# A hybrid convolution / RWKV-7 layer on one core: the score blocks' transposition cut in four, the weights' low parts made in two halves

## The chip, the core and the metric

The kernel runs on one core of one Trainium2 chip. A core has five engines that work side by side, each through its own list of instructions in order: TensorE (PE, matrix products; its weight loads are shown apart as PEld), VectorE (DVE), ScalarE (ACT), GpSimd (POOL) and SyncE (SP), which issues the transfers. The metric is the device time of one execution in microseconds, lower is better; the span in the profile is the time from the first to the last instruction of one profiled execution.

## The reference

One layer of a decoder is computed for 2048 new tokens of one sequence and for 8 short sequences of 4 tokens, which come with states. All is fp32, the model width is 1024:

```python
h = _rmsnorm(x, norm_g)
p = jnp.einsum('bsd,dn->bsn', h, w_in)
p_conv, p_rwkv, p_gate = _split(p, [N_CONV_COLS, N_RWKV_COLS, 2 * D_MODEL])
...
def step(S, inp):
    r_t, k_t, v_t, d_t, kk_t, a_t = inp
    sa = jnp.einsum('bhvk,bhk->bhv', S, -kk_t)
    S = (S * d_t[:, :, None, :] + sa[..., None] * (kk_t * a_t)[:, :, None, :]
         + v_t[..., None] * k_t[:, :, None, :])
    y = jnp.einsum('bhvk,bhk->bhv', S, r_t)
    return S, y
...
m = jax.nn.sigmoid(gc) * pc + jax.nn.sigmoid(gr) * pr
out = jnp.einsum('bsd,de->bse', m, w_o)
return x + out, new_conv, h[:, -1], S_fin.astype(S0.dtype)
```

A big projection feeds a gated convolution and an RWKV-7 branch of 16 heads, whose state is a 64 x 64 matrix for each head that every token decays and changes. Two output projections are gated, added, and projected once more.

## The kernel before, in words

**Precision.** A large product is done as three passes of a fast fp32 format: each operand X is split into a rounded high part and the rest, a low part, and high times high, low times high and high times low are added. For a weight block of 1024 x 128 the high part is a copy on ACT and the low part a subtraction on DVE (`whl<-wraw,whl` in the profile, `w_lows`). The first time a block is used both parts are stored to memory (`SP.store(keep, ...)`); the later sets read them back. There are 105 such subtractions, 81 of them for the input projection, most in the first quarter of the time.

**Sets, pairs, chunks.** The 2048 tokens are taken in four sets of 512; the last one also carries the short sequences. A set goes through 8 pairs of heads, so there are 32 pairs in all, and the recurrence of a pair runs over 8 chunks of 64 tokens. Inside a chunk the recurrence is rewritten with matrix products, and that needs the inverse of a lower triangular matrix of 64 x 64 for each head and chunk.

**The main stream.** PE's bulk is the projections (matmuls into `ip`, 24 for each block of 128 columns: 8 parts of the depth, three passes). `main_stream` walks them.

**The sides.** All other work is written as generators, which yield a weight after each step: `rwkv_keys` makes the scaled keys of a pair, `rwkv_solve` the inverse, `rwkv_merge` and `rwkv_load` put it and the transposed operands in place, `rwkv_chain` runs the eight chunks, `rwkv_out` normalises. They run one pair behind each other: while the chain of one pair runs, the inverse of the next one is solved. `drive` gives each side as much as its weight asks for after each projection matmul, if the planner (`Clock`, a running estimate of when each engine is free) says that what it needs is ready. So PE's order comes out as projections with small matmuls of the sides in between. The planner's costs for DVE depend on the number of elements, so more or smaller instructions shift its estimate and with it the places where the sides are let in. Afterwards the framework's own scheduler moves independent instructions of one engine past each other; what stands in the built program is shown below.

**The inverse.** In `rwkv_solve` two groups of score matmuls (`pt<-AR,BK`) are masked on DVE (`GM<-pt,mask_p`), ACT packs the diagonal blocks of 32 x 32 of eight chunks, two heads and two halves in `Mc`, and one DVE transposition of 128 x 1024 turns it into `Mi` (`Mi<-Mc`). Then 31 steps of a substitution follow on DVE, from row j = 31 down to 1, each with two instructions: a product (`tt<-Mi,X`), which reads row j of `Mi`, and a sum (`X<-X,tt`). A last transposition gives `Xo`.

**The chain.** Each chunk of `rwkv_chain` goes back and forth: PE multiplies the state (`pa<-S,AR`), DVE adds (`us<-pa,P`, two halves), PE multiplies with the inverse (`pb<-us,Xbd`), DVE and then ACT copy a half of the result each (`SV<-pb`), PE multiplies with the keys (`pb<-SV,BKt`), DVE updates the state (`S<-pb,pe,sp`, two halves), and the next chunk begins. Between two of these matmuls PE has only the projections that stand between them in its list.

Every operation is recorded through one helper, so all have line 121 in the profile; tiles tell them apart.

Of the kernel before, what the change touches and what calls it, by code (L numbers as in the profile page):

```python
# [7 lines left out]
F32 = mybir.dt.float32  # L8
# [3 lines left out]
ALU = mybir.AluOpType  # L12
# [4 lines left out]
P = 128  # L17
# [4 lines left out]
NCH = 8  # L22
# [4 lines left out]
W = {"sq": 1.0, "norm": 1.0, "lora": 2.0, "one": 1.0, "scan": 2.0, "exp": 2.0, "key": 1.0, "bones": 1.5,  # L27
     "sv": 1.5, "bt": 2.0, "score": 4.0, "inv0": 5.0, "inv": 0.45, "inv1": 4.0, "merge": 2.0,
     "gk": 1.3, "us": 1.3, "sa": 1.3, "state": 1.3, "samp": 2.0, "gn": 4.0, "out": 2.0}
# [150 lines left out]
def hybrid_kernel(tc, x_prompt, x_sample, state_conv, state_shift, state_rwkv, norm_g, w_in, conv_w,  # L180
# [5 lines left out]
    V, A, G, T = (Traced(e, n, clock) for e, n in ((nc.vector, "DVE"), (nc.scalar, "ACT"), (nc.gpsimd, "POOL"), (nc.tensor, "PE")))  # L186
# [4 lines left out]
    NB = D // P  # L191
# [57 lines left out]
    def w_lows():  # L249
        while lows:  # L250
            hl, raw, keep = lows.pop(0)
            V.tensor_tensor(out=hl[:, 1], in0=raw, in1=hl[:, 0].bitcast(F32), op=ALU.subtract)
            SP.store(keep, hl.bitcast(F32))

    def take_w(key):

        i = state["use"]
        assert order[i][0] == key, (order[i][0], key)
        state["use"] += 1
        w_advance(i + 1, i + 1, i + 1)  # L260
        w_lows()
        SP.flush(2)
        w_advance(i + 3, i + 2, i + WAHEAD)
        return parts_.pop(i)
# [211 lines left out]
    for q in range(2):  # L476
        V.tensor_tensor(out=mask_s[:, q, 0:NSAMP].rearrange("p (j i) -> p j i", i=SL),
                        in0=mask_p[:, q, 0:NSAMP].rearrange("p (j i) -> p j i", i=SL),
                        in1=seqm.unsqueeze(2).broadcast_to([P, NS, SL]), op=ALU.mult)
# [450 lines left out]
    def rwkv_solve(th, p, o):  # L930

        AR = o["AR"]
        samp = th == LAST
        GM = GMB[(th * NB + p) % 2]


        yield 0.0, (), 2
        for c0 in range(0, NCH + samp, 4):
            cs = range(c0, min(NCH + samp, c0 + 4))
            pp = [new_pt([P, 512], F32, name="pt") for _ in range(2)]  # L940
            for c in cs:
                for h in range(2):
                    T.matmul(pp[h][:, (c - c0) * P:(c - c0 + 1) * P], lhsT=BK[HS[h], c].rearrange("p q t -> p (q t)"),
                             rhs=AR[HS[h], c].rearrange("p q t -> p (q t)"), start=True, stop=True)
            k = len(cs)
            mk = mask_s if c0 == NCH else mask_p
            for h in range(2):
                V.tensor_tensor(out=GM[:, c0:c0 + k, :, h, :],
                                in0=pp[h][:, 0:k * P].rearrange("p (c a t) -> p c a t", a=2, t=64),
                                in1=mk.unsqueeze(1).broadcast_to([P, k, 2, 64]), op=ALU.mult)  # L950
            yield W["score"], (), 2 if c0 + 4 < NCH + samp else 0


        Mc = rw.tile([P, NCH, 32], F32, name="Mc")
        for i, g in enumerate(blk):
            h, b = i // 2, slice(i % 2 * 32, i % 2 * 32 + 32)
            A.copy(Mc[g], GM[b, 0:NCH, 0, h, b])
        yield 0.5, [Mc]
        Mi = rw.tile([P, 32, 32], F32, name="Mi")
        V.transpose(Mi.rearrange("p t (e c) -> p t e c", c=NCH),  # L960
                    Mc.rearrange("p c t -> p t c").unsqueeze(2).broadcast_to([P, 32, 4, NCH]))
        X = rw.tile([P, 8, 32], F32, name="X")
        A.copy(X, X0)
        Mo = rw.tile([P, NCH, 32], F32, name="Mo")
        A.copy(Mo[64:96], GM[0:32, 0:NCH, 0, 1, 32:64])
        yield W["inv0"], [Mi, X]

        for j in range(31, 0, -1):
            c0 = j // 4
            tt = sm.tile([P, 80], F32, name="tt")  # L970
            tv = tt[:, 0:(8 - c0) * j].rearrange("p (c i) -> p c i", i=j)
            V.tensor_tensor(out=tv, in0=Mi[:, j, 0:j].unsqueeze(1).broadcast_to([P, 8 - c0, j]),
                            in1=X[:, c0:8, j:j + 1].broadcast_to([P, 8 - c0, j]), op=ALU.mult)
            V.tensor_tensor(out=X[:, c0:8, 0:j], in0=X[:, c0:8, 0:j], in1=tv, op=ALU.add)
            yield W["inv"]
        Xo = rw.tile([P, 8, 4, 8], F32, name="Xo")
        V.transpose(Xo.rearrange("p a e c -> p (a e c)"), X.rearrange("p a b -> p (a b)"))
        o.update(GM=GM, Xo=Xo, Mo=Mo)
        yield W["inv"]
# [315 lines left out]
    for th in range(NSETS):  # L1295
        for p in range(NB):
            last = p == NB - 1
            k = 6 if th < LAST else (5 if not last else len(cg[th]))
# [143 lines left out]
    for th, hv, p, nx in plan:  # L1442
# [11 lines left out]
        e = EDGE / 2 * NB  # L1454
# [161 lines left out]
```

## Time and profile before

| what | value |
|---|---|
| median of 3 runs | 3207.14 us (3201.25 to 3209.92) |
| the profiled execution's own time | 3209.42 us |
| its span | 3207.7 us |
| PE busy | 3102.1 us (97%) |
| DVE busy | 1999.0 us (62%) |
| ACT busy | 1241.4 us (39%) |
| POOL busy | 309.9 us (10%) |
| mean granted TensorE clock | 0.991 |

PE is busy nearly all the time, so the time is PE's work and, beside it, the 105.6 us of the span (3207.7 - 3102.1) in which PE waited. A busy DVE costs nothing by itself; it costs where PE's next matmul waits for it. The columns of a group's row are: line, engine, operation, tile written <- tiles read, shapes, count | busy us, mean ns of one | idle us of the engine just before, and what ended it. In a timeline the first column is the start in us, the second the duration.

### The profile page before, as it was taken

How to read it: one execution, taken by the hardware profiler on the slowest of the kernel's cores; microseconds unless marked ns; L12 is line 12 of the kernel's file. 1: busy time of each engine (PE TensorE's matmuls, PEld its weight loads, DVE VectorE, ACT ScalarE, POOL GpSimd, SP SyncE). 2: the span in 40 equal slices, each digit the busy share in tenths (PEclk: the TensorE clock that was granted, in tenths of full speed). 3: DMA queues.
4: the chain of work that ended last, by engine and by line, in shares of the span. 5: the costliest groups of instructions: out<-in, count | busy, mean ns of one | idle time of the engine just before them, and what ended most of it. 6: DMA issues, size and time to landing. Idle time of an engine off the chain costs nothing. (4 is left out here: it accounts for less than half of the span.)

```text
span 3207.7 us, 55738 instructions
## 1 busy us (share of the span) xinstructions
PE 3102.1 (97%) x21594; PEld 2603.2 (81%) x21594; DVE 1999.0 (62%) x5712; ACT 1241.4 (39%) x2571; POOL 309.9 (10%) x517
## 2 busy tenths in 40 slices
PE   7999999999999999999999999999999999999998
PEld 6777777877777778777777799988898889778897
DVE  5687777776666666666666666776677654443332
ACT  5454554444433344444443444434344432211201
POOL 2011111110000001001110010000000000000000
PEclk9999999999999999999999999999999999999999
DMA  8786666644444444444444444343443469988863
GB/s 267 256 274 211 216 221 218 204 171 151 144 157 155 161 159 159 168 151 158 159 157 151 160 152 138 134 136 129 143 138 126 144 217 311 350 338 305 316 245 120
DMA packets 240991, 615.10 MB, mean 192 GB/s; under 512 B 33418, under 2 KB 143107, under 8 KB 186966
## 3 DMA queue, kind: packets, MB, share of 16 engines
q1 hardware_dynamic: 240582, 611.00, 55.5%
q8 instruction: 171, 2.80, 0.4%
q14 instruction: 94, 0.77, 0.1%
q0 software_dynamic: 144, 0.52, 0.0%
HBM read 452.10 MB, written 159.36 MB: 191 GB/s over the span
## 5 line engine op out<-in xcount | busy, mean ns | idle before, releaser
L121 PE MATMUL ip<-XH,whl 128*128 128x512 f32 (+3 forms) x7776 | 2107.3, 351 | 10.2 <-DVE gt L121 3.5
L121 PEld LDWEIGHTS ip<-XH,whl 128*128 128x128 f32 x7776 | 1341.8, 190 | 184.2 <-issue 30.4
L121 PE MATMUL ip<-XL,whl 128*128 128x512 f32 (+3 forms) x3888 | 1362.9, 351 | 2.6 <-POOL XL L121 2.6
L121 PEld LDWEIGHTS ip<-XL,whl 128*128 128x128 f32 x3888 | 738.5, 190 | 77.4 <-issue 6.2
L121 DVE TENSOR_TENSOR X<-X,tt 128x60 f32<-128x60 f32 (+24 forms) x992 | 211.7, 213 | 27.4
L121 DVE TENSOR_TENSOR tt<-Mi,X 128x60 f32<-128x60 f32 (+24 forms) x992 | 210.5, 212 | 28.0
L121 DVE SCALAR_TENSOR_TENSOR S<-pb,pe,sp 64x64 f32<-64x64 f32 x512 | 143.7, 281 | 100.7 <-PE pb L121 94.6
L121 ACT ACTIVATE sp<-S,pe 128x128 f32<-128x128 f32 x256 | 99.5, 399 | 264.2 <-DVE S L121 260.7
L121 ACT ACTIVATE tmp<-ip,vec 128x512 f32<-128x512 f32 (+2 forms) x174 | 103.2, 593 | 232.5 <-PE ip L121 231.1
L121 ACT COPY SV<-pb 64x64 f32<-64x64 f32 x256 | 53.3, 208 | 330.9 <-DVE SV L121 326.9
L121 PE MATMUL po<-whl,MH 128*128 128x512 f32 x544 | 170.6, 394 | 2.6 <-ACT whl L121 2.5
L121 DVE TENSOR_TENSOR whl<-wraw,whl 128x1024 fp32r<-128x1024 f32 x105 | 134.2, 1279 | 52.8 <-ACT whl L121 52.5
L121 DVE TENSOR_TENSOR us<-pa,P 64x64 f32<-64x64 f32 x512 | 110.3, 215 | 51.9 <-PE pa L121 39.8
L121 PEld LDWEIGHTS pb<-us,Xbd 128*128 128x128 f32 x512 | 86.3, 190 | 54.4 <-PE ip L121 20.8
L121 PE MATMUL ip<-RH,whl 128*128 128x512 f32 (+2 forms) x512 | 128.5, 341 | 1.1 <-DMA whl<-w_or 0.6
L121 PEld LDWEIGHTS pb<-SV,BKt 128*128 128x128 f32 x512 | 85.2, 189 | 54.0 <-ACT SV L121 45.3
L121 ACT CAST whl<-wraw 128x1024 fp32r<-128x1024 f32 x105 | 109.4, 1044 | 43.9 <-DMA wraw<-in_w_out_r_dram 14.0
L121 PEld LDWEIGHTS po<-whl,MH 128*128 128x128 f32 x544 | 102.1, 188 | 27.0 <-ACT whl L121 2.9
L121 PE MATMUL pb<-SV,BKt 128*128 128x128 f32 x512 | 107.1, 291 | 16.4 <-ACT SV L121 16.1
L121 DVE TENSOR_TENSOR GM<-pt,mask_p 128x512 f32<-128x512 f32 x128 | 82.4, 686 | 61.4 <-PE pt L121 61.4
L121 PE MATMUL pb<-us,Xbd 128*128 128x64 f32 x512 | 90.1, 258 | 22.5 <-DVE us L121 21.9
L121 ACT COPY Xbd<-Xo 32x256 f32<-32x256 f32 x128 | 88.2, 689 | 61.2 <-DVE Xo L121 59.1
(494 smaller groups left out, 3856.1 us busy)
## 6 DMA issues: line engine op xcount, KB each, us to landing
wraw<-in_w_in_dram SPq DMA_DIRECT2D x81, 512.0 KB
whl<-w_k SPq DMA_DIRECT2D x24, 1024.0 KB
whl<-w_r SPq DMA_DIRECT2D x24, 1024.0 KB
whl<-w_v SPq DMA_DIRECT2D x24, 1024.0 KB
whl<-w_z SPq DMA_DIRECT2D x24, 1024.0 KB
whl<-w_xin SPq DMA_DIRECT2D x24, 1024.0 KB
whl<-w_cg SPq DMA_DIRECT2D x24, 1024.0 KB
whl<-w_zc SPq DMA_DIRECT2D x24, 1024.0 KB
```

Source lines behind the costliest of these rows:

```text
L121: r = f(*a, **k)
```

## The change

In `w_lows` the low part of a weight block is made by two subtractions of 128 x 512 in place of one of 128 x 1024. In `rwkv_solve` the transposition of 128 x 1024 is cut in four of 128 x 256, each of which makes eight rows of `Mi` and is written into the loop of the substitution just ahead of the first step that reads one of them (j = 31, 23, 15 and 7). The weight that the transposition had for the planner, 5, is given out in five parts.

```diff
@@ w_lows
             hl, raw, keep = lows.pop(0)
-            V.tensor_tensor(out=hl[:, 1], in0=raw, in1=hl[:, 0].bitcast(F32), op=ALU.subtract)
+            for k in range(2):
+                c = slice(k * (NB // 2) * P, (k + 1) * (NB // 2) * P)
+                V.tensor_tensor(out=hl[:, 1, c], in0=raw[:, c], in1=hl[:, 0, c].bitcast(F32), op=ALU.subtract)
             SP.store(keep, hl.bitcast(F32))
@@ rwkv_solve
         Mi = rw.tile([P, 32, 32], F32, name="Mi")
-        V.transpose(Mi.rearrange("p t (e c) -> p t e c", c=NCH),
-                    Mc.rearrange("p c t -> p t c").unsqueeze(2).broadcast_to([P, 32, 4, NCH]))
         X = rw.tile([P, 8, 32], F32, name="X")
         A.copy(X, X0)
         Mo = rw.tile([P, NCH, 32], F32, name="Mo")
         A.copy(Mo[64:96], GM[0:32, 0:NCH, 0, 1, 32:64])
-        yield W["inv0"], [Mi, X]
+        yield W["inv0"] / 5, [X]
 
         for j in range(31, 0, -1):
+            if j % 8 == 7:
+                g = slice(j - 7, j + 1)
+                V.transpose(Mi[:, g].rearrange("p t (e c) -> p t e c", c=NCH),
+                            Mc.rearrange("p c t -> p t c")[:, g].unsqueeze(2).broadcast_to([P, 8, 4, NCH]))
+                yield W["inv0"] / 5, [Mi[:, g]]
```

The built program has 201 more DVE instructions (96 transpositions, 105 subtractions) and as many matmuls as before, but the orders differ on every engine. Three places show how.

The first is DVE in the first set, at the transposition of the third pair, while the chain of the second pair runs (`S`, `us` and `SV` belong to that chain). Before:

```order
L121 SCALAR_TENSOR_TENSOR S_472<-pb,pe,sp 64x64 x2
L121 STREAM_TRANSPOSE Mi<-Mc 128x1024
L121 TENSOR_TENSOR us<-pa,P_2452 64x64 x2
L121 TENSOR_TENSOR tt<-Mi,X 128x31
L121 TENSOR_TENSOR X<-X,tt 128x31
L121 COPY SV<-pb 64x64
```

With the change:

```order
L121 SCALAR_TENSOR_TENSOR S_472<-pb,pe,sp 64x64 x2
L121 STREAM_TRANSPOSE Mi<-Mc 128x256 x2
L121 TENSOR_TENSOR tt<-Mi,X 128x31
L121 TENSOR_TENSOR us<-pa,P_2528 64x64 x2
L121 TENSOR_TENSOR X<-X,tt 128x31
L121 STREAM_TRANSPOSE Mi<-Mc 128x256
L121 COPY SV<-pb 64x64
L121 TENSOR_TENSOR tt<-Mi,X 128x30
L121 STREAM_TRANSPOSE Mi<-Mc 128x256
```

The addition `us` stood behind the whole transposition and now stands behind two pieces and one product; all four pieces stand within the first three products and sums, not seven steps apart as they are written.

The second is DVE in the second set, at the transposition of the sixth pair, while the chain of the fifth runs. Before:

```order
L121 SCALAR_TENSOR_TENSOR S_474<-pb,pe,sp 64x64 x2
L121 TENSOR_TENSOR cv<-ip,cv 128x512
L121 TENSOR_TENSOR us<-pa,P_10297 64x64 x2
L121 STREAM_TRANSPOSE Mi<-Mc 128x1024
L121 COPY SV<-pb 64x64
L121 TENSOR_TENSOR tt<-Mi,X 128x31
```

With the change:

```order
L121 SCALAR_TENSOR_TENSOR S_474<-pb,pe,sp 64x64 x2
L121 TENSOR_TENSOR cv<-ip,cv 128x512
L121 TENSOR_TENSOR us<-pa,P_10414 64x64 x2
L121 STREAM_TRANSPOSE Mi<-Mc 128x256 x2
L121 TENSOR_TENSOR tt<-Mi,X 128x31
L121 STREAM_TRANSPOSE Mi<-Mc 128x256
L121 TENSOR_TENSOR X<-X,tt 128x31
L121 COPY SV<-pb 64x64
```

The copy `SV` stood behind one transposition and now stands behind three of the four pieces, a product and a sum.

The third is PE at the last chunk of the chain of the fifth pair of the second set, from the product with the inverse (`pb<-us`) to the product with the keys (`pb<-SV`). Before:

```order
L121 MATMUL pb<-us,Xbd_208 128x64
L121 MATMUL ip<-XH,whl 128x512
L121 MATMUL ip<-XL,whl 128x512
L121 MATMUL ip<-XH,whl 128x512 x2
L121 MATMUL ip<-XL,whl 128x512
L121 MATMUL ip<-XH,whl 128x512 x2
L121 MATMUL ip<-XL,whl 128x512
L121 MATMUL pb<-SV,BKt 128x128
```

With the change:

```order
L121 MATMUL pb<-us,Xbd_208 128x64
L121 MATMUL ip<-XH,whl 128x512 x2
L121 MATMUL ip<-XL,whl 128x512
L121 MATMUL pb<-SV,BKt 128x128
L121 MATMUL ip<-XH,whl 128x512 x2
```

Eight projection matmuls stood between the two products and three do now; the other five have moved behind the second one. On DVE seven instructions of the substitution stand between `us` and `SV` of this chunk in both programs, and seven in place of six between the `S` before it and `us`. The chains of the second to sixth pair of the second and of the third set, ten in all, have this same place.

## The prediction

> **What bounds the kernel now.** I read the shares of the engines first, then the stretches of the span, then PE's own waits, and last the order of time around three of these waits.
>
> ```profile
> PE 3102.1 (97%) x21594; PEld 2603.2 (81%) x21594; DVE 1999.0 (62%) x5712; ACT 1241.4 (39%) x2571; POOL 309.9 (10%) x517
> 300.00:600.00 300.00, 289.56 (x1790) 226.01 (x1789) 229.38 (x612) 147.88 (x273) 38.75 (x56) 1.00 0.68 219
> 1200.00:1500.00 300.00, 294.60 (x2041) 238.50 (x2039) 191.90 (x556) 123.02 (x258) 34.47 (x59) 0.99 0.45 157
> 2100.00:2400.00 300.00, 292.39 (x2559) 266.87 (x2558) 216.22 (x703) 120.71 (x299) 24.24 (x42) 1.00 0.41 137
> ```
>
> The stretches give width, then PE, PEld, DVE, ACT and POOL busy. PE is the bound everywhere; it is idle for 10.4 us of 300 in the first set, 5.4 where the second goes over to the third, 7.6 in the last. DVE has 70 us of 300 free even in the first set. So DVE's total is not what is paid for, and the change does not touch PE's matmuls. What can move is how long PE stands at a matmul that waits for DVE.
>
> ```profile
> PE pb L121 <- DVE us L121: 21.9, 37, 1.6
> PE pb L121 <- ACT SV L121: 16.1, 26, 1.4
> PE ip L121 <- DVE whl L121: 1.9, 2, 1.1
> ```
>
> Here (us in total, times, longest) PE's two long waits are the chain's: for `us`, and for `SV`, whose second half ACT copies after DVE's. The third row is all that PE ever waited for the low parts of the weights.
>
> **The change part by part.** First DVE's busy time, from groups by form:
>
> ```profile
> L121 DVE TENSOR_TENSOR whl<-wraw,whl 128x1024 fp32r<-128x1024 f32 x105 | 134.2, 1279 | 52.8 <-ACT whl L121 52.5
> L121 DVE STREAM_TRANSPOSE Mi<-Mc 128x1024 f32<-128x1024 f32 x32 | 65.6, 2050 | 8.0 <-ACT Mc L121 7.5
> L121 DVE STREAM_TRANSPOSE Xo<-X 128x256 f32<-128x256 f32 x32 | 14.1, 440 | 0.5
> L121 DVE TENSOR_TENSOR RL<-yraw,RH 128x512 fp32r<-128x512 f32 x16 | 10.8, 689 | 13.5 <-ACT RH L121 13.5
> ```
>
> *Low parts.* A subtraction of 128x512 to the same format takes 0.689 us (last row), so two take 1.378 where one took 1.279: 0.10 us more for 105 blocks, 10 us of DVE. It is hidden where DVE is idle, as above; if it were not, it would cost at most these 10 us. The gain is that PE can start on the first half and that the chain's small operations can slip between the halves. PE's direct wait is 1.9 us in two cases; I take -1.5, with 0 and -3 as ends.
>
> *Transposition, its price.* No row shows a 128x256 piece with this access. Lower end: `Xo`, a transposition of that size, 0.440 us. Upper end: a quarter of `Mi` and the same 0.10 us for each of three cuts, (2.050 + 0.30) / 4 = 0.59 us. Four pieces are then 1.76 to 2.36 us for 2.05, -9 to +10 us of DVE in all, hidden as above. I take the middle, 0.52, since `Mi` reads a strided, repeated source and `Xo` a dense one.
>
> The Trainium skill, page "VectorE: DVE Perf Modes", section "The TRN2 errata — SBUF-src ops pay a fixed extra latency per instruction", speaks against pieces: a large tile pays a fixed latency once and many small tiles pay it each, so tiles should have 512 elements or more; it names about 150 cycles at 0.96 GHz, an estimate of 0.16 us. By it a piece would take (2.05 + 3 x 0.16) / 4 = 0.63 us, and three pieces ahead of `SV` would add about 2 us over ten pairs to the sum below; by the `Xo` row they would take off as much. No run here shows it for this operation, and the sum takes neither.
>
> *Transposition, where it blocks the chain.* In the first set `us` stood right behind it:
>
> ```profile
> 257.31 2.05 DVE L121 STREAM_TRANSPOSE Mi<-Mc 128x1024 f32<-128x1024 f32 x1 [0.61 <-ACT Mc L121]
> 259.39 0.45 DVE L121 TENSOR_TENSOR us<-pa,P 64x64 f32<-64x64 f32 x2
> 259.99 0.41 PE L121 MATMUL pb<-us,Xbd 128*128 128x64 f32 x2 [1.13 <-DVE us L121]
> ```
>
> PE waited 1.13 us here. With the change two pieces and a product stand ahead, 2 x 0.52 + 0.21 = 1.25 us for 2.05: the wait shrinks to some 0.3 us. Six pairs of the first set have such a wait beside their transposition; in two of them the new order lets `us` through as here, in the others it still has two or three pieces ahead or behind the `S` before it. I take -0.5 us for each, -3 (ends 0 and -6).
>
> In the ten pairs of the second and third set that the order's second place stands for, `SV` stood behind the transposition:
>
> ```profile
> 1104.06 2.08 DVE L121 STREAM_TRANSPOSE Mi<-Mc 128x1024 f32<-128x1024 f32 x1
> 1106.04 0.19 DVE L121 COPY SV<-pb 64x64 f32<-64x64 f32 x1
> 1106.53 0.49 PE L121 MATMUL pb<-SV,BKt 128*128 128x128 f32 x2
> ```
>
> PE wanted this product about 0.14 us earlier (its projection before it began at 1106.15, and such starts are 0.23 apart). Now three pieces, a product and a sum stand ahead: 3 x 0.52 + 0.42 = 1.98 us for 2.08. I take 0, with -1.4 (the wait gone, ten times) and +1 (3 x 0.59 + 0.42 = 2.19) as ends. So cutting does not free the chain here: the pieces stand together, because all four depend on nothing but `Mc`, and the scheduler takes them as early as it can.
>
> *The projections under the chain.* This is what I think decides. The planner's new costs move where the chain is let in. At the third place of the order PE had eight projections between `pb<-us` and `pb<-SV`, and now has three. What the path on DVE takes there is in the trace of before:
>
> ```profile
> 1115.62 0.45 DVE L121 TENSOR_TENSOR us<-pa,P 64x64 f32<-64x64 f32 x2
> 1116.10 0.24 DVE L121 TENSOR_TENSOR tt<-Mi,X 128x75 f32<-128x75 f32 x1
> ...
> 1117.70 0.22 DVE L121 TENSOR_TENSOR tt<-Mi,X 128x60 f32<-128x60 f32 x1
> 1117.84 0.21 DVE L121 COPY SV<-pb 64x64 f32<-64x64 f32 x1
> 1116.26 0.36 PE L121 MATMUL pb<-us,Xbd 128*128 128x64 f32 x2
> 1118.38 0.45 PE L121 MATMUL pb<-SV,BKt 128*128 128x128 f32 x2
> 1118.08 0.21 ACT L121 COPY SV<-pb 64x64 f32<-64x64 f32 x1 [0.55 <-DVE SV L121]
> ```
>
> Seven instructions of the substitution (1116.10 to 1117.84) stand ahead of the copy, ACT's half follows until 1118.29, and the product could start at about 1118.35. Eight projections fill 1116.26 to 1118.38, so PE waited for nothing. Five fewer, at 0.233 us each (the distance of starts in a row of projections), bring PE to the product at 1117.2, and the operand still comes at 1118.35: a wait of 1.1 to 1.2 us. The kernel before has one place of this kind in the same pairs, with three projections and a 1.5 us subtraction in DVE's list:
>
> ```profile
> 1092.76 1.52 DVE L121 TENSOR_TENSOR tmp<-tmp 128x512 fp32r<-128x512 f32 x1
> 1092.95 0.34 PE L121 MATMUL pb<-us,Xbd 128*128 128x64 f32 x2
> 1093.41 0.62 PE L121 MATMUL ip<-XH,whl 128*128 128x512 f32 x2
> 1094.71 0.49 PE L121 MATMUL pb<-SV,BKt 128*128 128x128 f32 x2 [0.67 <-ACT SV L121]
> ```
>
> Three projections end the cover at about 1093.87; the product came at 1094.71, 0.84 us late. So a step costs 0.84 to 1.2; I take 1.1, ten pairs: +11. The seventh instruction between `S` and `us` of the same chunk (0.25 us each, seven from 1116.10 to 1117.84) delays `pb<-us`, which had no slack: +0.25 x 10 = +2.5. Together +13.5, ends +8 (ten times 0.84) and +15 (ten times 1.2 + 0.25). Nothing takes this back later: the five projections are done after the product, where PE does not wait for the chain any more.
>
> *First and last set.* There the whole order differs. I counted the chain's steps with less than 1.5 us of matmuls under them (matmuls in the order by the distances of their starts): in the second to seventh pair of the first set 14 of 138 before and 40 now; in the last set 39 and 59. A short step costs nothing if DVE's list is short there, and 0.84 us if it is as long as at 1092.76. I take 0.2 us for each of the 46 more: +5 and +4. The ends are 0 and 0.6, so 0 to +28 for both. Where the third set goes over to the last, two waits for `us` behind a transposition, of the kind at 259.99, go as well: -1.5.
>
> *Sum.* -1.5 (low parts) -3 (first set's `us`) + 0 + 13.5 + 5 + 4 - 1.5 = +16.5 us. The profiled execution took 3209.4 us around its span of 3207.7 and would take 3225.9; it lay 2.3 above the median of the runs, 3207.14, so I predict 3224.
>
> **The rivals.**
>
> *Faster.* The chain's small operations go ahead between pieces and halves. For it: all waits for `us` sum to 21.9 us, and the longest stand behind the transposition. Against it: only six pairs of the first set and two of the last have them there, and PE's short steps take more back. If the short steps cost a third of what I take (7.5 for 22.5) and the waits behind `Mi` and the low parts shrink by twice what I take (-12), it is -4.5: 3203; if the short steps cost nothing at all, -12: 3195. The point from which it decides is 0.27 of my price for a short step, where the sum is zero.
>
> *No change.* The steps that lost projections wait, but DVE gets as far ahead meanwhile, so that the next wait of the chain is shorter by as much. For it: only DVE's extra 1 to 20 us would be left, all hidden: 3207. Against it: at the end of a chain no further step of that chain follows. That the change does not do what it says belongs here: the pieces do not stand between the steps, so `SV` waits as long as before, and if the short steps were also harmless, the time would be the same.
>
> *Much slower: DVE becomes the bound in the first set.* DVE has 70.6 us of 300 free there; four pairs with at most 0.3 us more and some 30 weight blocks with 0.1 add 4 us. It would have to fall behind by bursts. If short steps in the first and last set cost 0.6 us each, the sum is +35: 3242.
>
> **How the numbers follow.** Forecast (short steps starve PE) 0.58, faster 0.13, no change 0.25, much slower 0.04. Differences of 0.3%, about 9.6 us, are what a measurement of this kernel can tell from no change. The forecast's own range is 3217 to 3240. The range is 3201 to 3240: it takes in no change and half of the faster case. Faster 0.13, same 0.25, slower 0.62.
>
> **What would show it.** PE's wait `pb` for `ACT SV` grows from 16.1 us and its count from 26 by at least ten; ten waits of about 1.1 us stand at the last chunk in the second and third set, where the stretch 1200 to 1500 loses 5 us or more of PE's busy time. The wait for `us` shrinks in the first set. A piece takes 0.44 to 0.59 us, a half about 0.69. I am wrong if the wait for `SV` stays near 16 us, or if the second and third set take as long as before.

## The result: slower by 1.6%

The changed kernel takes 3259.04 us (median, 3253.2 to 3263.3) where the kernel before takes 3207.66 in the same comparison: a ratio of 1.0159 [1.0146, 1.0171], +51.4 us. The forecast was 3224, +16.5, with 3240 as the upper end. The profiled execution of the changed kernel took 3253.2 us around a span of 3251.5, the lowest of its runs, so the traces below account for +43.8 us (3251.5 - 3207.7) of the 51.4.

The shares of the engines after, and the three stretches that were shown of before:

```profile
PE 3119.7 (96%) x21594; PEld 2612.7 (80%) x21594; DVE 2000.4 (62%) x5913; ACT 1242.3 (38%) x2571; POOL 301.9 (9%) x517
300.00:600.00 300.00, 290.16 (x1849) 226.93 (x1844) 223.12 (x623) 151.05 (x278) 33.33 (x54) 1.00 0.68 214
1200.00:1500.00 300.00, 289.15 (x2017) 234.06 (x2016) 188.41 (x586) 121.32 (x254) 34.09 (x59) 0.99 0.46 159
2100.00:2400.00 300.00, 292.83 (x2605) 268.23 (x2603) 192.45 (x658) 122.87 (x296) 26.46 (x41) 0.99 0.41 136
```

DVE is as busy as before (2000.4 us for 1999.0). PE is idle for 131.8 us of the span (3251.5 - 3119.7) where it was for 105.6, +26.2. And PE is *busy* for 17.6 us more, with the same 21594 matmuls. The loss has these two halves.

**The waits.** PE's waits after (us in total, times, longest):

```profile
PE pb L121 <- ACT SV L121: 24.7, 35, 1.9
PE pb L121 <- DVE us L121: 17.6, 35, 1.7
PE pa L121 <- DVE S L121: 8.3, 14, 1.2
PE ip L121 <- DVE wraw L121: 8.0, 1, 8.0
PE ip L121 <- DVE gt L121: 6.1, 1, 6.1
PE pt L121 <- DVE T L121: 5.0, 5, 1.1
PE ip L121 <- DVE whl L121: 2.9, 2, 2.3
```

and the rows of before that the prediction did not show:

```profile
PE ip L121 <- DVE gt L121: 3.8, 2, 3.5
PE pt L121 <- DVE T L121: 2.7, 4, 1.1
PE pa L121 <- DVE S L121: 2.6, 5, 0.9
```

`SV` +8.6, the new wait for `wraw` +8.0, `pa` +5.7, `gt` and `T` +2.3 each, `whl` +1.0, `us` -4.3: together +23.6 of the +26.2.

**The busy time.** One group of matmuls explains nearly all of it: the scores, `pt<-AR,BK`, by form, before and then after.

```profile
L121 PE MATMUL pt<-AR,BK 64*128 64x128 f32 x1056 | 79.0, 286 | 0.1
```

```profile
L121 PE MATMUL pt<-AR,BK 64*128 64x128 f32 x1056 | 95.2, 287 | 0.0
```

The same 1056 records, each as long as before (286 and 287 ns), cover 16.2 us more: they overlap less. The experiments show why.

**The last chunk.** The third place of the order that the change showed, in the timeline of the changed kernel (one of the ten pairs; PE, DVE and ACT rows, start and duration first):

```profile
1061.50 0.22 DVE L121 TENSOR_TENSOR us<-pa,P 64x64 f32<-64x64 f32 x1
1061.75 0.23 DVE L121 TENSOR_TENSOR tt<-Mi,X 128x70 f32<-128x70 f32 x1
...
1061.99 0.33 PE L121 MATMUL pb<-us,Xbd 128*128 128x64 f32 x2
...
1062.12 0.70 PE L121 MATMUL ip<-XH,whl 128*128 128x512 f32 x2
...
1062.66 0.40 PE L121 MATMUL ip<-XL,whl 128*128 128x512 f32 x1
...
1063.47 0.21 DVE L121 COPY SV<-pb 64x64 f32<-64x64 f32 x1
...
1063.71 0.21 ACT L121 COPY SV<-pb 64x64 f32<-64x64 f32 x1 [1.20 <-DVE SV L121]
...
1063.97 0.49 PE L121 MATMUL pb<-SV,BKt 128*128 128x128 f32 x2 [0.91 <-ACT SV L121]
```

Three projections, then 0.91 us in which PE stands: what the prediction drew. Measured in its way, from where the next projection would have started (1062.66 + 0.23), the product is 1.08 us late. All ten places show such a wait, of 0.89 to 0.91 us, and the stretch from 1200 to 1500 lost 5.45 us of PE's busy time (294.60 to 289.15), as the prediction said. One more place repeats in the same ten chains, which it did not name, the product with the inverse in the chunk before:

```profile
1055.91 0.41 PE L121 MATMUL pb<-us,Xbd 128*128 128x64 f32 x2 [0.42 <-DVE us L121]
```

Ten waits of 0.40 to 0.42 us stand there, about 4 us.

**What the prediction did not see.** In the first set PE stands 8 us at the transposes of the short sequences' rows (timeline of the changed kernel):

```profile
119.22 2.42 POOL L121 TENSOR_TENSOR rstd<-nw,mhalf 128x13 f32<-128x13 f32 x1 [2.85 <-DVE nw L121]
121.68 0.17 DVE L121 TENSOR_TENSOR nw<-rstd 128x13 f32<-128x13 f32 x1 [2.39 <-POOL rstd L121]
...
122.67 0.74 DVE L121 TENSOR_SCALAR wraw<-wraw,rstd 32x1024 f32<-32x1024 f32 x1
...
123.46 1.07 PE L121 MATMUL ip<-ident,wraw 40*128 40x40 f32 x8 [7.97 <-DVE wraw L121]
```

These transposes stand behind 408 projections in the new order and stood behind 498 before, where nothing waited for them. Their step yields without naming a tile to wait for, so the planner issues it wherever its weight comes up, and the weights had moved.

### The profile page after: what moved, and what is told of

Same layout as the page of the kernel before. It is cut to its first block, busy times and chain, and to the rows that moved or that the text cites. A ratio compares the mean times of both kernels' runs of the same rounds, so it can differ in the third digit from the quotient of the medians.

```text
span 3251.5 us, 55906 instructions
## 1 busy us (share of the span) xinstructions
PE 3119.7 (96%) x21594; PEld 2612.7 (80%) x21594; DVE 2000.4 (62%) x5913; ACT 1242.3 (38%) x2571; POOL 301.9 (9%) x517
## 5 line engine op out<-in xcount | busy, mean ns | idle before, releaser
L121 DVE TENSOR_TENSOR X<-X,tt 128x60 f32<-128x60 f32 (+24 forms) x992 | 211.1, 213 | 25.9
L121 DVE TENSOR_TENSOR tt<-Mi,X 128x60 f32<-128x60 f32 (+24 forms) x992 | 209.8, 211 | 25.9
L121 DVE SCALAR_TENSOR_TENSOR S<-pb,pe,sp 64x64 f32<-64x64 f32 x512 | 143.5, 280 | 97.8 <-PE pb L121 91.7
L121 DVE TENSOR_TENSOR whl<-wraw,whl 128x512 fp32r<-128x512 f32 x210 | 143.8, 703 | 36.7 <-ACT whl L121 34.8
L121 PE MATMUL pb<-SV,BKt 128*128 128x128 f32 x512 | 106.8, 290 | 25.0 <-ACT SV L121 24.7
L121 PEld LDWEIGHTS po<-whl,MH 128*128 128x128 f32 x544 | 102.1, 188 | 24.7 <-DVE whl L121 0.9
L121 PEld LDWEIGHTS pa<-S,AR 128*128 128x128 f32 x512 | 87.2, 188 | 33.6 <-DVE S L121 21.3
L121 PE MATMUL pa<-S,AR 128*128 128x128 f32 x512 | 103.4, 283 | 8.5 <-DVE S L121 8.3
```

Of the source, the lines that this page charges most:

```text
L121: r = f(*a, **k)
```

## The experiments

Every kernel was compared with the kernel before on its own chip; the differences below are to the median of that comparison, and the changed kernel's is +51.4.

| kernel | ratio to before [95%] | us |
|---|---|---|
| plan_of_before: new instructions, old order | 0.9987 [0.9978, 0.9996] | -3.1 |
| plan_of_after: old instructions, new order | 1.0147 [1.0130, 1.0164] | +50.0 |
| lows_only | 1.0027 [1.0016, 1.0038] | +6.8 |
| mi_only | 1.0109 [1.0094, 1.0124] | +38.1 |
| pieces_once | 1.0000 [0.9991, 1.0009] | +1.0 |
| five_yields | 1.0052 [1.0035, 1.0069] | +19.7 |
| first_only | 1.0050 [1.0035, 1.0065] | +15.3 |
| middle_only | 1.0065 [1.0047, 1.0083] | +21.4 |
| last_only | 1.0032 [1.0019, 1.0045] | +10.2 |
| hurry_last_chunk | 1.0025 [1.0015, 1.0034] | +8.9 |
| weight_first | 1.0144 [1.0125, 1.0162] | +47.2 |
| late_due | 1.0119 [1.0104, 1.0134] | +40.2 |
| c1_74_after | 1.0072 [1.0057, 1.0087] | +25.5 |
| late_c1 | 1.0041 [1.0025, 1.0057] | +13.9 |
| c1_74_before | 1.0128 [1.0109, 1.0146] | +41.5 |
| heads_apart | 1.0068 [1.0050, 1.0085] | +24.0 |
| alternate | 1.0107 [1.0090, 1.0124] | +36.6 |
| between_halves | 0.9977 [0.9968, 0.9987] | -7.6 |

### Order or instructions

Two kernels cross the instructions with the order. Both tell the planner one thing and issue another. The old instructions in the new order:

```diff
 # w_lows and rwkv_solve of the changed kernel
-                V.tensor_tensor(out=hl[:, 1, c], ...)            # two halves
+                clock.add("DVE", [hl[:, 1, c]], ..., 150 + 1.05 * (NB // 2) * P)
+            nc.vector.tensor_tensor(out=hl[:, 1], ...)           # one whole
-                V.transpose(Mi[:, g]..., ...)                    # a piece
+                clock.add("DVE", [Mi[:, g]], [Mc], 150 + 1.6 * 256)
+                if j == 31:
+                    nc.vector.transpose(Mi..., ...)              # the whole
```

> The whole transposition and the whole subtractions of before, emitted untold to the planner, which is told the costs of the pieces and halves and goes through the five yields: the order of the changed kernel (17091 of 17946 matmuls at the same place in PE's list) with the instructions of before. Theory 'order': 3240 to 3262 us, and the ten waits at the last chunk stay. Theory 'pieces': 3203 to 3218 us.

The new instructions in the old order (the two edits the other way round):

> The pieces and halves of the change, emitted untold to the planner, which is told the costs of the whole instructions and yields as before: the order of before (17298 of 17946 matmuls at the same place) with the instructions of the change. Theory 'order': 3198 to 3220 us, since DVE's 23 us more of work are hidden. Theory 'pieces': 3235 us or more.

Measured: +50.0 and -3.1 us. The order makes the whole loss. The 201 further instructions cost nothing; this kernel is even a little faster, by 0.13%. So everything that follows asks what in the order it is.

### Which part of the change

> The weights' low parts in two halves, the transposition whole as before. Theory 'order': the loss comes from where the planner now puts the chain's matmuls in PE's list. In this program the chain's steps with less than 1.5 us of matmuls under them are as many as before (24, 44 and 37 in the first, the two middle and the last set, before 24, 44 and 37; with the whole change 43, 57 and 56), so the time is 3198 to 3218 us, about that of before (3207.7). Theory 'pieces': the smaller DVE instructions themselves are at fault; then the 105 cut subtractions carry a share of the 51 us, and the time is 3225 us or more.

> The transposition in four pieces with the five yields, the low parts whole as before. Theory 'order': short steps are 40, 57 and 55, as with the whole change, so 25 to 45 us of the loss are here: 3233 to 3253 us, with ten waits of about 1.06 us at the last chunk in the second and third set. The transposes of the short sequences' rows stand behind 472 projections (498 before, 408 with the whole change), so PE's single wait of 8.0 us for them should be gone or small. If halves and pieces only cost DVE's time and nothing of the order, 3210 to 3225.

`lows_only` is the first hunk of the diff alone, `mi_only` the rest. +6.8 and +38.1: the pieces bring most of it. The loss of `lows_only` is not the chain's, whose short steps are as many as before: its score matmuls cover 90.3 us for 79.0, while PE's wait for `us` fell from 21.9 to 13.1. `mi_only` has no wait for `wraw`, so its 38.1 owe nothing to that one. The pieces consist of an edit of costs and one of yields, which two more kernels take apart:

```diff
 # pieces_once: kernel before, all four pieces in the old place, one yield
-        V.transpose(Mi..., ...)
+        for j in range(31, 0, -8):
+            g = slice(j - 7, j + 1)
+            V.transpose(Mi[:, g]..., Mc...[:, g]...)
         yield W["inv0"], [Mi, X]
```

> The kernel before with the transposition in four pieces at the old place, all at once and known to the planner, one yield behind them as before, low parts whole. The planner counts 4 x 150 + 1638 = 2238 ns for them where it counted 1788. In the order the ten last chunks keep 2.08 us of projections, but the short steps of the first set count 36 for 24. Theory 1, the loss is in the order and comes from the pieces' places among the steps: 3210 us (3205 to 3214), no waits of 1 us at the last chunk. Theory 2, any further instruction that the planner counts scatters the order: 3230 to 3245 us as with the pieces in the loop.

```diff
 # five_yields: kernel before, whole transposition, the weight in five parts
-        yield W["inv0"], [Mi, X]
+        yield W["inv0"] / 5, [X]
         for j in range(31, 0, -1):
+            if j % 8 == 7:
+                yield W["inv0"] / 5, [Mi[:, j - 7:j + 1]]
```

> The kernel before with its transposition whole, at its old place and cost; only its weight is given out in five yields at the places of the change, each naming the rows it would wait for. In the order the short steps count 24, 53 and 37 for 24, 44 and 37, and the ten last chunks keep their 2.08 us of projections. Theory 1, it takes yields and pieces together, since only a piece that is due later moves the chain: 3207 to 3210 us. Theory 2, the yields alone move the order and make the loss: 3235 us or more.

The pieces alone: +1.0, as the first theory said, but not because nothing moved:

```profile
PE pb L121 <- DVE us L121: 4.7, 8, 1.2
L121 PE MATMUL pt<-AR,BK 64*128 64x128 f32 x1056 | 88.0, 286 | 0.9 <-DVE GM L121 0.9
```

PE's wait for `us` fell from 21.9 to 4.7 us. Other waits took 10 us of this back, so that PE's idle time is 98.5 us (3206.8 - 3108.3) for 105.6, and the score matmuls cover 9.0 us more. A gain at the chain and a loss elsewhere cancel, and both come with the new order: `plan_of_before` has the same pieces, and there PE waits 15.3 us for `us` and the score matmuls cover 79.3.

The yields alone: +19.7, which neither theory had. The count of short chain steps moved in the middle sets only, 53 for 44. PE's waits name the place:

```profile
PE pt L121 <- DVE T L121: 17.5, 17, 1.5
```

```profile
909.66 0.21 PE L121 MATMUL pt<-T,Mo 32*32 32x32 f32 x1 [1.04 <-DVE T L121]
```

The second row is from its timeline. Seventeen waits of about 1.04 us stand where the finished inverse is put in place (`rwkv_merge`), which were four. The share of the solve's weight that is paid out later has pushed PE's merge matmuls ahead of DVE's transposition `T`. It is the same kind of damage as the last chunk's, in another place: a pair repeats the pair before it, so one bad place is paid ten or more times.

### Which part of the program

The change in one set at a time:

```diff
+        cut = th == 0                # middle_only: 0 < th < LAST; last_only: th == LAST
+        if not cut:
+            V.transpose(Mi..., ...)  # the whole, as before
-        yield W["inv0"] / 5, [X]
+        yield (W["inv0"] / 5, [X]) if cut else (W["inv0"], [Mi, X])
-            if j % 8 == 7:
+            if cut and j % 8 == 7:
```

> The change in the first set alone (pieces there; the halves of the low parts everywhere, nearly all of which are made in that set). In the order the first set is as in the changed kernel (45 short steps, the set-up's transposes behind 408 projections) and the other sets are as in the kernel before (44 and 37). Theory 1, the time at equal numbers of projections tells where the loss lies (16.6 us of 43.6 by the end of the first set): 3224 us (3218 to 3230). Theory 2, the prediction's terms for this set, -1.5 - 3 + 5: 3208 us.

> The four pieces in the second and third set alone, low parts whole. Middle sets: 60 short steps for 44, nine of the ten last chunks with 0.92 us of projections for 2.08; the other sets as in the kernel before. Theory 1, by the time at equal numbers of projections (17.8 us between the end of the first set and the end of the third): 3225 us. Theory 2, the prediction's term, ten waits of 1.1 and 0.25 at the operand before: +13.5, 3221 us at most, 3219 by nine of them. Theory 3, the steps behind a wait get it back: 3207 to 3211 us.

> The four pieces in the last set alone, low parts whole. Last set: 55 short steps for 37; the other sets as in the kernel before. Theory 1, by the time at equal numbers of projections (9.2 us from the end of the third set on): 3217 us. Theory 2, the prediction's terms, +4 for short steps and -1.5 for two waits: 3210 us. With the other two kernels of this call: if the three parts are independent, their losses add up to 51 us within 7.

Measured +15.3, +21.4 and +10.2; the sum is 46.9 of 51.4. The sets are nearly independent, and each loses more than the prediction's terms for it (0.5, 13.5 and 2.5). Their score matmuls cover 91.7, 79.0 and 82.5 us, for 79.0 before: the middle sets lose mostly by waits (PE's idle time is 123.3 us for 105.6), the first and the last by both.

### The ten waits alone

```diff
 # rwkv_chain of the kernel before, pairs 2 to 6 of the second and third set
+                fast = c == NCH - 1 and (th * NB + p) % 8 in range(1, 6) and 0 < th < LAST
-                yield W["sa"], [SV[0:64, c, :]]
+                yield (W["sa"] * 0.0, []) if fast else (W["sa"], [SV[0:64, c, :]])
...
-                yield W["state"], [S]
+                yield W["state"] + W["sa"] * (1 - 0.0) * fast, [S]
```

> The kernel before with one thing of the changed order alone: in the chains of the second to sixth pair of the second and third set the step that issues the last chunk's product with the keys names no operand to wait for and carries no weight (the next step carries it), so that four projections (1.15 us) stand ahead of this product in place of nine (2.08 us). The rest of the order is as before. Theory 1, each of the ten waits costs its length and nothing pays it back: operand ready some 2.0 us after the step begins, ten times 0.83 us, 3216 us, and PE's wait for SV grows from 16 to 24 us. Theory 2, PE gets the wait back at a later step of the chain or of the next pair: 3208 us within 3, though the wait for SV grows as much.

+8.9 us [+4.8, +10.9 by the interval of the ratio], and PE's waits are

```profile
PE pb L121 <- ACT SV L121: 23.6, 36, 1.4
PE pb L121 <- DVE us L121: 21.8, 37, 1.6
```

for 16.1, 26 and 21.9, 37: ten waits more, 7.5 us more. PE's idle time in all grew by 8.8 us (3217.6 - 3103.2 = 114.4 for 105.6), so nothing pays them back. The reverse, lifting them in the changed kernel, is not worth as much:

```diff
 # weight_first: the changed kernel
-        yield W["inv0"] / 5, [X]
+        yield W["inv0"], [X]
...
-                yield W["inv0"] / 5, [Mi[:, g]]
+                yield 0.0, [Mi[:, g]]
```

> The changed kernel, but the weight of the transposition, 5, is given whole before the loop and the four pieces yield with weight 0, still waiting for their rows. In the order the first set is as in the changed kernel (43 short steps), the last set nearly (57 for 56), and the last chunk of the ten pairs has ten projections (2.31 us) under it in place of three (0.92 us); the middle sets count 65 short steps for 57. Theory 1, the ten waits of 1.06 us are a cost of their own: 3249 us, and PE's wait for SV falls from 24.7 us by about 10. Theory 2, the other steps of the same chains pay for it, eight more of them being short: 3259 us within 3, and the wait for SV or us grows elsewhere by as much.

```profile
PE pb L121 <- DVE us L121: 22.3, 47, 1.7
PE pa L121 <- DVE S L121: 14.3, 24, 1.2
PE pb L121 <- ACT SV L121: 14.0, 20, 1.9
```

`SV` falls by 10.7 us, and `pa` grows by 6.0 and `us` by 4.7: the sum is unchanged, and the time with it within 4.2 us (the second theory). In `hurry_last_chunk` the projections left the chain's time, since they went behind its last product. Here the chain's share is fixed, and what the last chunk gets, other steps lose: ten of the new waits for `us`, 0.42 or 0.43 us each, stand in the same last chunks.

### A wider share for the chain, and a later set-up

```diff
-CUTS = {"most": (0.7, 0.0, 0.0, 0.34, 0.7, 0.95, 0.95), ...
+CUTS = {"most": (0.74, 0.0, 0.0, 0.34, 0.7, 0.95, 0.95), ...
```

> The changed kernel, but the chains of the first three sets are given 0.74 of their pair's time in place of 0.70. In the order the last chunk of the ten pairs then has nine projections (2.08 us) under it in place of three (0.92 us); the first set's order is the same up to there, and the short steps count 43, 55 and 54 in the first, the middle and the last set for 43, 57 and 56. Theory 1, the ten last-chunk waits of 1.06 us are 10 us of the loss: 3249 us, and the stretch from 1200 to 1500 gets back 3 us or more of PE's busy time. Theory 2, the wait is made up by the chain's steps that are now pressed or late elsewhere: 3259 us within 3.

> A control for the changed kernel with the chains' share at 0.74: the kernel before with 0.74 in place of 0.70. In the order the short steps count 24, 34 and 53 for 24, 44 and 37; the last chunks keep 2.08 us. Theory 1, the wider share repairs what the change broke, and the kernel before has nothing of it to repair: 3207 us within 5. Theory 2, a wider share helps any order, since each step of the chain gets more projections: 3190 to 3197 us, and then most of the 25 us that it gave the changed kernel say nothing about the change.

```diff
 # late_due: set-up of the short sequences, ahead of the transposes of their rows
+        yield 0.0, [xt[0:m]]
```

> The changed kernel, but the set-up of the short sequences yields once more, with its normalised rows as what it waits for, so that the planner holds back the transposes of these rows: they stand behind 469 projections in place of 408 (498 in the kernel before). Theory 1, single waits add up: the wait of 8.0 us for wraw goes and nothing comes back, 3251 us, the wait for the short sequences' transposes under 0.5 us. Theory 2, a wait that goes comes back, because PE then meets DVE's list at its next step: 3259 us, and the first 300 us lose as much of PE's busy time as in the changed kernel.

> The changed kernel with both: the set-up of the short sequences held back until its rows are ready, and the chains' share at 0.74. Short steps 49, 55 and 54. If the two gains lie in different places and add: 3259.0 - 10.7 - 25.3 = 3223 us. If the gain of the set-up was not its own but a chance reshuffling of the first set: anything from 3223 to 3240 us. What is left above 3207 us is the first set's and the last set's.

The wider share takes the changed kernel from +51.4 to +25.5, far more than the ten waits. PE's idle time fell by 13.0 us (131.8 to 118.8) and its busy time by 9.0 (3119.7 to 3110.7), of which the score matmuls are 2.2; where the other 6.8 went, these runs do not show. The row for `SV`, which was 24.7, 35:

```profile
PE pb L121 <- ACT SV L121: 8.2, 13, 1.9
```

But the same number makes the kernel *before* 41.5 us slower, which neither theory had. Its longest row of waits and one of them from its timeline:

```profile
PE pt L121 <- DVE Yc L121: 27.7, 20, 1.9
```

```profile
903.07 0.66 PE L121 MATMUL pt<-ident,BK 128*128 128x128 f32 x4 [1.94 <-DVE Yc L121]
```

The chain now ends later, and the next pair's operands (`rwkv_load`) meet a buffer that its output still holds: one more place of the same kind. So 0.74 is no better number; each number goes with one order.

The later set-up gives 11.2 us, but not as the first theory had it (waits of PE, then the timeline):

```profile
PE pb L121 <- DVE us L121: 12.3, 30, 1.7
PE ip L121 <- ACT whl L121: 9.1, 2, 8.6
```

```profile
122.70 0.17 DVE L121 TENSOR_TENSOR nw<-rstd 128x13 f32<-128x13 f32 x1 [2.39 <-POOL rstd L121]
...
126.31 0.65 ACT L121 COPY Xbd<-Xo 32x256 f32<-32x256 f32 x1 [8.22 <-DVE Xo L121]
...
129.57 1.04 ACT L121 CAST whl<-wraw 128x1024 fp32r<-128x1024 f32 x1
...
130.67 1.52 PE L121 MATMUL ip<-XH,whl 128*128 128x512 f32 x2 [8.58 <-ACT whl L121]
```

These are two rows of PE's waits and four of the timeline. The wait of 8.0 us for `wraw` is gone, and one of 8.6 us for a weight block stands in its place, as the second theory had it: DVE still waits for POOL's `rstd` in the last steps of an inverse, ACT stands 8.2 us for that inverse, and the copy of the weight block is queued behind on ACT. What PE waits less lies in the chain's steps of the first set, `us` and `pa` (in all 17.6 to 12.3, 8.3 to 4.6), which the shift happened to help. PE's whole idle time fell by 16.0 us (131.8 to 115.8), and its busy time grew by 9.9, of which the score matmuls are 0.6; the rest stays unexplained. Both edits together give 37.5 us, where 25.9 and 11.2 add up to 37.1.

### The score matmuls

In `rwkv_solve` eight score matmuls of a group are written alternating between the two heads. One head's operands lie in the lower 64 rows of PE's array, the other's in the upper 64. In the built program of before they alternate in nearly all of the 64 groups. In the changed one most groups of the first set are torn: two of one head, another matmul, two more, projections, four of the other head. From the timeline of PE, one group of before (16 records are eight matmuls), and then the pieces in which the groups of a pair start in the changed kernel:

```profile
327.86 1.16 PE L121 MATMUL pt<-AR,BK 64*128 64x128 f32 x16
```

```profile
340.49 0.71 PE L121 MATMUL pt<-AR,BK 64*128 64x128 f32 x4
...
341.56 0.71 PE L121 MATMUL pt<-AR,BK 64*128 64x128 f32 x4
...
343.32 1.71 PE L121 MATMUL pt<-AR,BK 64*128 64x128 f32 x16
```

The test breaks the alternation alone, in the kernel before and its order:

```diff
-            for c in cs:
-                for h in range(2):
-                    T.matmul(pp[h]..., lhsT=BK[HS[h], c]..., rhs=AR[HS[h], c]..., ...)
+            for h in range(2):
+                for c in cs:
+                    nc.tensor.matmul(pp[h]..., ...)       # the planner counts them as before
```

> The kernel before and its order, but the eight score matmuls of a group are issued head by head (four of the lower rows, then four of the upper) in place of alternating, and the planner counts them as before. Theory 1, such a group takes 1.71 us for 1.16 (both lengths are in the trace of the change in the first set alone): 66 groups by 0.55 us, +36 us, 3244 us, with the group's busy time at 115 us for 79.0 and PE's waits as before (SV and us together 38 us within 3). Theory 2, the order of the heads costs nothing: 3208 us.

```profile
L948 PE MATMUL pt<-AR,BK 64*128 64x128 f32 x1056 | 113.9, 286 | 0.4 <-DVE wraw L121 0.3
325.30 1.71 PE L948 MATMUL pt<-AR,BK 64*128 64x128 f32 x16
```

(This kernel issues them from a line of their own, 948; by the traces 21380 of PE's 21594 records have the same tiles at the same place in the order as in the kernel before.) The group grows by 34.9 us (36 expected for 66 groups; for the 64 of eight matmuls it would be 35) and the time by 24.0: two thirds. PE's idle time is 103.5 us (3225.9 - 3122.4) for 105.6, and its busy time without this group is 14.6 us shorter than before (3122.4 - 113.9 for 3102.1 - 79.0). The profiled execution had a mean granted clock of 0.994, that of before 0.991; how much of the 14.6 this makes, these runs don't show. The Trainium skill, page "TensorEngine Tiling (Array Packing)", section "Tiling Modes", says that different tiles of the array can load weights and multiply in parallel. The trace agrees as far as 1.16 us alternating and 1.71 us head by head go.

Restored in the changed kernel:

```diff
-                    T.matmul(pp[h]..., ...)
+                    i = T.matmul(pp[h]..., ...).ins
+                    if last is not None:
+                        tc.add_manual_dep(i, last.name, ...)   # issue order only, no wait
+                    last = i
```

> The changed kernel, with each score matmul of a group queued behind the one before it as written, so that the two heads, which lie in the lower and the upper 64 rows of the array, alternate again; the first matmul of 14 groups of the first set now stands alone ahead of some projections. The planner's order is else that of the changed kernel (46, 57, 57 short steps for 43, 57, 56). Theory 1, the same matmuls take longer when one head's stand together: the group pt<-AR,BK falls from 95.2 us towards the 79.0 of the kernel before, less some for the matmuls that stand alone, 3247 us (3243 to 3252). Theory 2, the group's longer time is a matter of the records and the loss lies in the waits alone: 3259 us within 3.

+36.6 for +51.4: 14.8 us back, as the first theory said, but its reason carries a part only. The group fell from 95.2 to 89.8 us, 5.4 of the 16.2, since the first matmul of most groups of the first set now stands alone; the wait for `us` fell by 3.1 (17.6 to 14.5) and that for `pa` by 1.6 (8.3 to 6.7). The two profiled executions are 11.0 us apart (3251.5 and 3240.5), so the rest of the 14.8 is not in these traces.

### Pieces that are really apart

In the new order the four pieces stand together, because each depends on `Mc` alone. Here they write to two buffers in turn, so that the third must wait until the first one's rows are read. The planner is told the costs of the whole instructions, so that the order is that of before (by the traces 21401 of PE's 21594 records have the same tiles at the same place), and the halves of the low parts are in.

```diff
+        def piece(j):
+            Mi[j // 8] = rw.tile([P, 8, 32], F32, name="Mi", bufs=2)
+            nc.vector.transpose(Mi[j // 8]..., Mc...[:, j - 7:j + 1]...)
+        piece(31)
...
+            if j in (23, 15, 7):
+                piece(j)
```

> The order of the kernel before, with the low parts in two halves and the transposition in four pieces, neither known to the planner; the pieces write to a pool of two buffers, so that the third can begin only when the rows of the first have been read, and the pieces do stand some 20 instructions apart. Theory 1, the size of DVE's instructions is worth next to nothing, since DVE is idle a third of the time: 3204 us (3200 to 3207), as with the four pieces standing together (3203.8). Theory 2, pieces that are truly apart free the chain: under 3197 us, with PE's waits for SV and us together under 30 us where they were 38.0.

-7.6 us, 0.9977 [0.9968, 0.9987]: faster than both kernels. That is the edge of the first theory's range and not the second's, since `us` and `SV` still cost 37.5 us (20.8 and 16.7) for 38.0. What the change set out to do, with the halves, is worth a quarter of a per cent once the order is held.

## Why the prediction was wrong in size

The direction was right, and so was the mechanism of the ten last chunks. What failed is the price of the first and the last set, which was sought in the chain's short steps alone, and the sentence that PE's matmuls are not touched.

- **"The change does not touch PE's matmuls."** This is the sentence that failed first. Their number is the same, but the same score matmuls cover 16.2 us more, because the new order tears the two heads apart, and the sum had no term for it. The count of matmuls was taken for their time. What this costs is known roughly: `heads_apart` lost 24.0 us of time for 34.9 of such busy time, which would make some 11 of the 16.2, an estimate; in `pieces_once` 9.0 us of it came with shorter waits and a loss of 1.0.
- **Low parts, -1.5.** A half takes 0.703 us (predicted 0.689) and is hidden; but PE's wait for `whl` rose from 1.9 to 2.9, and the halves alone made +6.8 by the order that they brought. The term priced the instruction and not the planner's answer to it.
- **Price of a piece.**

```profile
L121 DVE STREAM_TRANSPOSE Mi<-Mc 128x256 f32<-128x256 f32 x128 | 78.8, 632 | 10.0 <-ACT Mc L121 9.5
L121 DVE TENSOR_TENSOR whl<-wraw,whl 128x512 fp32r<-128x512 f32 x210 | 143.8, 703 | 36.7 <-ACT whl L121 34.8 <-DMA wraw<-in_x_prompt_dram 1.1
```

  A piece takes 0.632 us, outside 0.44 to 0.59. Four cost 2.53 us for 2.05, 0.16 for each of three cuts, where the prediction took 0.10 from a subtraction: I took the fixed cost of one operation from another. The Trainium skill's rule on page "VectorE: DVE Perf Modes", section "The TRN2 errata — SBUF-src ops pay a fixed extra latency per instruction", gave an estimate of 0.63, and the trace agrees. Nothing hung on it: `plan_of_before` has the same pieces and is not slower.
- **First set's `us`, -3, and the two waits before the last set, -1.5.** Both hold. Up to the end of the first set's chains (757 us before, 775 after) the wait for `us` fell from 11.2 to 6.1 us, and the two waits of 1.20 and 0.83 us (at 1871 and 1965 us before) are gone. In all it fell by 4.3 only, mainly because of the ten new waits in the chunk before the last.
- **Ten last chunks, +13.5.** The mechanism and its price hold: 1.08 us for 1.1, and put alone into the kernel before, with one projection more, +8.9 where 8.3 was worked out. "Nothing takes this back later" holds there too. The 2.5 for `pb<-us` does not: PE waits at that product in none of the ten last chunks (1061.99 above is one), but about 4 us in the chunk before.
- **Short steps, +5 and +4.** The term that was mis-sized. 0.2 us for each of 46 steps looked for the loss of the first and the last set only in the chain. The first set lost 15.3 where its terms gave 0.5: one wait of 8.0 us in the set-up, which no term had, and 12.7 us more of score matmuls, while the chain's wait for `us` fell. The last lost 10.2 for 2.5, with 3.5 us more of score matmuls. The count does not tell the price: by its expectation `pieces_once` has 36 short steps in the first set for 24, and its wait for `us` is the shortest of all these runs. The middle sets had no term for short steps beside the last chunks: of their 16 further ones (60 for 44 in `middle_only`) nine are these. To the 8 us between 13.5 and 21.4 the waits in the chunk before contribute, and those for `T` and at `pa`, which grew by 2.9 and 2.7 us (5.6 and 5.3); no run takes these apart.
- **The rivals.** The faster one is what the instructions do by themselves (-3.1, and -7.6 when the pieces are apart), and the order outweighs it some sixteen times. The gain that it meant, 17.2 us less waiting for `us`, does stand in `pieces_once`, and is lost there elsewhere. "No change", by which DVE gets ahead meanwhile, fell with `hurry_last_chunk`. "Much slower" had a time nearer the truth, 3242, for a reason that fell: DVE's busy time did not grow, and `plan_of_after`, without one extra instruction, is as slow.
- **The range** ended at 3240 because it allowed only for the terms that had a name. An order that changes on every engine has more places than the three that the sum was built on.

What stays open: why the heads are torn apart in the first set and, less, in the last, but not in the middle ones; what a torn group costs in time, since `heads_apart` lost two thirds of the extra busy time and `pieces_once` almost nothing; and how the 51.4 us divide exactly, since single edits move several of these places at once.

## What to carry to other kernels

When a planner derives the order from costs, first hold the order and change the instructions, then hold the instructions and change the order: two runs tell which of the two is being measured, and here the order was worth +50 us and the instructions -3. Read a new order for every place that a steady pair repeats, not for the chain alone: each such place cost 1 to 2 us ten or more times, and three different edits (the yields, the chain's share, the pieces with their yields) each brought out another one. And compare the busy time of groups whose count is equal: where small matmuls run side by side, their order is part of their price.

## What was not expected of the hardware

- Eight score matmuls that alternate between the lower and the upper 64 rows of the array take 1.16 us; head by head they take 1.71 us, and four of one head alone (8 records) take as long as all eight alternating, 1.16 us in the trace of the change in the first set:

```profile
347.19 1.16 PE L121 MATMUL pt<-AR,BK 64*128 64x128 f32 x8
```

- The cost of cutting a DVE instruction is not one number, not even for one operation. By the mean of its records each cut of the strided transposition costs 0.16 us (4 x 0.632 - 2.050, over three cuts), and that of the subtraction 0.13 us in the changed kernel (2 x 0.703 - 1.279), but 0.21 us in `plan_of_before` (2 x 0.745 - 1.279):

```profile
L255 DVE TENSOR_TENSOR whl<-wraw,whl 128x512 fp32r<-128x512 f32 x210 | 152.4, 745 | 51.7 <-ACT whl L121 49.9 <-DMA wraw<-in_w_out_c_dram 0.8
```

  By the time that the groups cover in the changed kernel it is less, 0.14 us ((78.8 - 65.6) / 96) and 0.09 us ((143.8 - 134.2) / 105).
